# A list scheduler's model of the core: table loads, scan time, exponential pace and latencies changed, and the work ordered anew

## The chip, the cores and the metric

The kernel runs on all eight cores of one Trainium2 chip. Each core computes one of the eight batch elements with the same program; the cores exchange nothing. The metric is the device time of the slowest core, in microseconds (us). Cores 0 to 3 lie on one die and cores 4 to 7 on the other.

For every run there is the span of each core and the mean clock that was granted to its TensorE (1.0 is full speed). In some runs some cores were granted less (0.934 to 0.952 on four in one of the kernel before); the slowest core then tells of the clock.

Engines: PE is TensorE (PEld its weight loads), ACT is ScalarE, DVE is VectorE, POOL is GpSimd, SP issues the DMAs.

## The reference

A hybrid decoder layer, cut to what matters:

```python
D_MODEL = 1024; BATCH = 8; SEQ = 4096
h = rms_norm(x, g_pre); proj = h @ w_in                  # 5648 columns
# mixer A: causal differential attention with ALiBi, 4 heads, two 64-wide maps per head
pd = softmax(s1) - lam * softmax(s2); oa = pd @ v
ya = (rms_norm(oa) * silu(za)) @ w_up_a
# mixer B: gated linear attention (GLA), 4 heads; the decay is the "gate" of this document
glog = log_sigmoid(lr @ w_alpha + b_alpha) / 16
b = cumsum(glog) within a chunk; exp(b), exp(-b) scale q and k
yb = (rms_norm(ob) * silu(zb)) @ w_up_b
y = sigmoid(gate_a) * ya + sigmoid(gate_b) * yb
out = x + rms_norm(y @ w_out, g_post)
```

## The kernel before

The kernel works through eight tiles of 512 tokens. It isn't written as one sequence for each engine. It declares some 15,000 operations, each with a guess of its time (`occ`, how long it holds its engine, and `tail`, how long after that its result is there), and a greedy list scheduler puts them in order, picks an engine where there is a choice, and writes one fixed instruction queue per engine. On the chip each queue ran in that one order, with waits on semaphores: in the trace of the kernel before, the 1169 instructions of ACT, the 2272 of DVE and the 303 of POOL come in the same order on all eight cores. A wrong guess costs nothing by itself; it costs when it puts something in front of a queue that is not ready (3.58 us of PE in the example below).

The core of the scheduler:

```python
SEM_LAT = 0.14
...
        while len(order) < len(ops):
            best = None
            for e in ENGS:
                for o in avail[e]:
                    st = o.ready if o.ready > free[e] else free[e]
                    if len(o.alts) > 1 and any(max(o.ready, free[a]) + o.alts[a][0] < st + o.alts[e][0] for a in o.alts):
                        continue                     # another engine would finish it earlier
                    # ... (cut: buffers) ...
                    key = (st, o.prio, o.idx)        # earliest start first, then priority
                    if best is None or key < best[:3]:
                        best = (st, o.prio, o.idx, o, e)
            # ... (cut) ...
            occ, tail = o.alts[e]
            if e == "pe" and o.mode != pe_mode:
                st += 0.1                            # change of the array's tiling mode
                pe_mode = o.mode
            o.eng, o.start = e, st
            free[e] = st + occ
            o.fin = free[e] + tail                   # (cut: DMAs)
            # ... when the last dependency d of s is placed:
                        if d.eng == "pe" and "pe" in s.alts:
                            t = d.start
                        else:
                            t = d.fin + SEM_LAT
```

The times, and a copy that may go to DVE or to ACT:

```python
def _dve(n, rate=1.0, scalars=0):
    return (0.068 + 0.06 * scalars + n / rate / 960.0, 0.095)
def _act(n, psum=False):
    return ((0.051 if psum else 0.093) + n / 1200.0, 0.115)
...
copy(lambda t=t, s=s: hT[t % 2][:, :, s * 128:(s + 1) * 128], lambda b=b: ptr(b), [b], [f"hT{t % 2}_{s}"], 1024, bf_in=True)   # engs=("dve", "act")
```

The GLA gate, once per tile, is a serial piece (lambdas cut):

```python
P.op({"act": _act(512, True)}, ... func=AF.Exp, scale=-1.0, bias=nbal ...)      # twice
P.op({"act": _act(1024)},      ... func=AF.Ln, bias=1.0 ...)
P.op({"dve": _dve(512)},       ... tensor_tensor_scan ...)                      # twice
P.op({"act": _act(1024)},      ... func=AF.Exp, scale=-1.0 / 16.0 ...)
P.op({"act": _act(1024)},      ... func=AF.Exp, scale=1.0 / 16.0 ...)
```

All the sigmoids and silus are Tanh activations. In the trace below (core 5) Exp follows Tanh 127 times and Ln five times without a table load, but between Tanh and Ln there is always one, of 1283 ns: every tile but the first has a load before its Ln, and every tile has one before the next Tanh. Two PSUM buffers (`pg`) carry all projections, so PE stops when ACT or DVE is late in reading one: on this core it waited 5.1 us in eight waits until DVE had read one into `szB` (L643), and 2.4 us in five until it had at L904.

The softmax here doesn't subtract the row's maximum and nothing guards it: scores larger than these inputs give would overflow.

## Time and profile before

The median of the first three runs is 1463.7 us (1461.4 to 1464.9). The profiled run is fast, with all eight cores between 1448.2 and 1456.4 us at a clock of 0.987 to 0.991.

The first lines of the page (busy time, share of the span, instruction count) of the kernel before, slowest core, core 5:

```profile
span 1456.4 us, 31339 instructions; the slowest of 8 cores (1448.2 to 1456.4 us)
...
PE 1368.1 (94%) x11280; PEld 757.7 (52%) x11280; DVE 771.0 (53%) x2272; ACT 848.8 (58%) x1169; POOL 203.8 (14%) x303
...
PE 85%; DVE 5%; issue 3%; DMA 3%; ACT 3%; POOL 0%; SPq 0%; DVEq 0%; ACTq 0%; POOLq 0%
```

The last line is the chain of waits by engine. PE bounds the kernel, and a busy PE hides stalls inside its busy time (1368 us busy, against 1323 us of pure issue in the table below). So I went through the matmul records one by one: from the start of one to the start of the next, less columns/2.4 GHz + 2.5 ns and 95 ns when the tiling mode changes. The remainder is what I call stall. The three constants are read from this trace: 216 ns for 512 columns and 56 ns for 128, so 2.4 columns a ns and 2.5 ns; and 312 ns in place of 216 (median) after 512 columns when a 64-row matmul comes next, so about 95 ns for the change of mode.

| core 5, before | us |
|---|---|
| pure issue of 11280 matmuls, with 623 mode changes (59 us) | 1323 |
| stall, all | 113 |
| of it in the first 150 us | 34 |
| of it after 1340 us | 18 |
| of it in eight stretches of 14 us, from 3 us before each Ln | 39 |
| of it in single stalls of 1 us or more (28 of them) | 47 |

The groups of instructions of the kernel before, with operation, count, busy time and mean ns of one. They give the table loads, the scan and the exponential:

```profile
L814 ACT ACTIVATE sb_PT<-ps_qk 128x1024 bf16<-128x1024 f32 x480 | 472.0, 1022 | 198.6 <-PE ps_qk L806 194.1 <-PE ps_acc L486 3.5
...
L642 ACT ACT_TABLE_LOAD x8 | 10.3, 1283 | 2.3 <-PE ps_pg L486 2.2
L697 ACT ACT_TABLE_LOAD x7 | 9.0, 1283 | 0.2
...
L700 DVE TENSOR_TENSOR_SCAN sb_cum<-sb_rmask,sb_gl 128x512 f32<-128x512 bf16 x16 | 18.7, 1211 | 10.1 <-ACT sb_gl L697 10.1
```

The sixteenth load is the first instruction of ACT (L623), and the first Ln has none before it. Fifteen loads come from the change between Ln and Tanh: they are gone in e7, where Ln is replaced by Tanh. After each of the 16 loads the next activation starts 11 or 12 ns later, so a load holds ACT for about 1.30 us (387.85 to 389.15 us below). Now the gate of the third tile in order of time (start, length, engine, line, operation; in brackets how long the engine sat idle and what ended it). First ACT, then PE, of the kernel before, core 5:

```profile
387.85 1.28 ACT L697 ACT_TABLE_LOAD   x1
389.15 1.06 ACT L697 ACTIVATE sb_gl<-sb_gl 128x1024 f32<-128x1024 f32 x1
390.22 1.28 ACT L642 ACT_TABLE_LOAD   x1
391.52 0.60 ACT L642 ACTIVATE sb_tmp<-ps_pg 128x512 f32<-128x512 f32 x1
392.01 1.02 ACT L814 ACTIVATE sb_PT<-ps_qk 128x1024 bf16<-128x1024 f32 x1
392.91 1.03 ACT L478 ACTIVATE sb_hT<-ps_pg 128x1024 bf16<-128x1024 bf16 x1
393.82 1.07 ACT L702 ACTIVATE sb_gl<-sb_cum 128x1024 f32<-128x1024 f32 x1
```

```profile
389.56 0.96 PE L486 MATMUL ps_acc<-sb_V,sb_PT 128*128 128x129 bf16 x14
394.09 1.24 PE L486 MATMUL ps_pg<-sb_wbuf,sb_hT 128*128 128x512 bf16 x5 [3.58 <-ACT sb_hT L478]
395.17 3.54 PE L486 MATMUL ps_pg<-sb_hT,sb_wbuf 128*128 128x512 bf16 x8
398.49 0.68 PE L486 MATMUL ps_pg<-sb_wbuf,sb_hT 128*128 128x512 bf16 x2
```

PE waits 3.58 us for a copy into `hT`, which stands in ACT's queue behind Ln, a second table load, a Tanh and an exponential. The model thought that ACT would be free two table loads earlier and gave it the copy. After the wait eight matmuls take 3.54 us, that is 427 ns from one to the next instead of 216: the clock record of this core is 0.5 from 395.2 to 398.7 us.

The same eight stretches, as a table by stretch (busy us and instructions of PE, PEld, DVE, ACT and POOL, then granted clock, share of DMA and GB/s) of the kernel before, four of the eight rows and the sum of all eight:

```profile
386.00:400.00 14.00, 10.43 (x81) 5.44 (x79) 8.54 (x22) 11.20 (x14) 2.16 (x3) 0.88 0.36 128
...
724.00:738.00 14.00, 10.52 (x73) 5.39 (x72) 6.79 (x20) 11.85 (x14) 1.74 (x3) 0.88 0.19 71
910.00:924.00 14.00, 9.94 (x89) 5.50 (x87) 7.08 (x20) 11.75 (x14) 2.20 (x3) 0.89 0.13 53
1110.00:1124.00 14.00, 10.19 (x106) 6.15 (x104) 5.12 (x8) 13.18 (x15) 0.64 (x1) 1.00 0.15 63
...
sum 112.00, PE 86.36 PEld 45.77 DVE 63.99 ACT 87.90 POOL 12.66; mean PE 10.79 PEld 5.72 DVE 8.00 ACT 10.99 POOL 1.58
```

The first number after the length, 14.00, is PE: 10 to 10.5 us of 14 are busy in these four (10.8 in the mean of all eight), in a kernel where PE is busy 94% of the time. A clock of 0.88 means that a quarter of the stretch ran at half (0.5 from 395.2 to 398.7 us in the first row, from 733.2 to 736.6 in the second).

### The profile page before, as it was taken

The page shows a single profiled execution, that of the slowest core. Times are in us where ns is not written, and L with a number is a line of the kernel's source. Part 1 is how long each engine was busy: PE and PEld are TensorE (multiplying, and loading weights), DVE is VectorE, ACT ScalarE, POOL GpSimd, SP SyncE. Part 2 cuts the span into 40 slices and gives each one's busy share as a digit, 9 for nine tenths or more (in the row PEclk, how much of TensorE's full clock was granted, in tenths as well). Part 3 has the DMA queues.
Part 4 walks back from the last instruction along what each step waited for, and adds up shares of the span by engine and source line. Part 5 has one row for each costly group of instructions (what it writes and reads, how often), then busy time and mean ns, then how long its engine had stood idle before and what let it go on. Part 6 is the DMA issues. An engine that isn't in the chain of part 4 may idle for free.

```text
span 1456.4 us, 31339 instructions; the slowest of 8 cores (1448.2 to 1456.4 us)
## 1 busy us (share of the span) xinstructions
PE 1368.1 (94%) x11280; PEld 757.7 (52%) x11280; DVE 771.0 (53%) x2272; ACT 848.8 (58%) x1169; POOL 203.8 (14%) x303
## 2 busy tenths in 40 slices
PE   4997898999899999999999999899998999999896
PEld 2344444545455555555555555466555666655532
DVE  4589567645665465644565435563354543334734
ACT  4356455436644466546765667656677667777511
POOL 1025121101110021101111111010010110101100
PEclk9999999999999999999999999999999999999998
DMA  9999795243523253333512335222243221224133
GB/s 275 291 275 258 228 315 181 80 153 146 174 89 144 88 214 108 114 136 131 198 59 106 113 111 206 76 88 88 88 160 131 88 88 59 88 88 146 59 145 116
DMA packets 54279, 207.54 MB, mean 143 GB/s; under 512 B 6880, under 2 KB 15472, under 8 KB 39152
## 3 DMA queue, kind: packets, MB, share of 16 engines
q1 hardware_dynamic: 54128, 205.54, 41.4%
q8 instruction: 93, 1.52, 0.4%
q14 instruction: 58, 0.48, 0.1%
HBM read 173.01 MB, written 32.51 MB: 141 GB/s over the span
## 4 chain that ended last, share of the span: by engine, by line
PE 85%; DVE 5%; issue 3%; DMA 3%; ACT 3%; POOL 0%; SPq 0%; DVEq 0%; ACTq 0%; POOLq 0%
PE ps_pg L486 57%; PE ps_acc L486 16%; PE ps_qk L806 9%; PE ps_pg L490 2%; DMA sb_KT<-w_out 1%; ACT sb_PT L814 1%; DMA sb_wbuf<-wsc 1%; DVE sb_gatedB L777 1%; ACT L642 1%; DVE sb_cum L700 0%; DMA sb_KT<-w_up_a 0%; DVE sb_junkd L768 0%; DMA sb_xa<-x 0%; DVE sb_szB L643 0%; DVE sb_xr L934 0%
## 5 line engine op out<-in xcount | busy, mean ns | idle before, releaser
L814 ACT ACTIVATE sb_PT<-ps_qk 128x1024 bf16<-128x1024 f32 (+1 forms) x544 | 518.9, 997 | 215.7 <-PE ps_qk L806 209.8
L486 PE MATMUL ps_pg<-sb_hT,sb_wbuf 128*128 128x512 bf16 x1664 | 448.5, 387 | 10.3 <-DVE sb_V L523 1.8
L486 PE MATMUL ps_acc<-sb_V,sb_PT 128*128 128x129 bf16 x4224 | 427.9, 220 | 10.3 <-ACT sb_PT L814 6.8
L486 PEld LDWEIGHTS ps_acc<-sb_V,sb_PT 128*128 128x128 bf16 x4224 | 312.9, 98 | 148.4 <-issue 40.3
L486 PE MATMUL ps_pg<-sb_wbuf,sb_hT 128*128 128x512 bf16 x960 | 247.0, 382 | 13.6 <-ACT sb_hT L478 5.5
L486 PEld LDWEIGHTS ps_pg<-sb_hT,sb_wbuf 128*128 128x128 bf16 x1664 | 155.0, 99 | 161.0 <-issue 45.2
L904 DVE SCALAR_TENSOR_TENSOR sb_tmp<-sb_tmp,ps_pg 128x512 f32<-128x512 f32 x128 | 87.6, 685 | 212.2 <-PE ps_acc L486 138.4
L806 PE MATMUL ps_qk<-sb_QT,sb_KT 64*128 64x256 bf16 (+1 forms) x2176 | 162.6, 268 | 4.9 <-ACT sb_PT L814 4.7
L889 ACT ACTIVATE sb_tmp<-ps_pg 128x512 f32<-128x512 f32 x128 | 76.5, 598 | 108.7 <-PE ps_pg L486 71.9
L486 PEld LDWEIGHTS ps_pg<-sb_wbuf,sb_hT 128*128 128x128 bf16 x960 | 88.0, 98 | 98.8 <-issue 26.3
L486 PE MATMUL ps_pg<-sb_wbuf,sb_yT 128*128 128x512 bf16 x480 | 122.6, 386 | 5.0 <-DMA sb_wbuf<-wsc 3.4
L858 POOL TENSOR_TENSOR sb_statE<-sb_statE,sb_mhalf 128x1 f32<-128x1 f32 x128 | 76.0, 599 | 358.3 <-DVE sb_statE L856 344.9
L806 PEld LDWEIGHTS ps_qk<-sb_QT,sb_KT 64*128 64x128 bf16 x2176 | 83.9, 94 | 73.3 <-issue 55.9
L819 POOL TENSOR_SCALAR_AFFINE_SELECT sb_PT<-sb_PT 128x512 bf16<-128x512 bf16 x64 | 44.8, 700 | 507.4 <-ACT sb_PT L814 507.4
L642 ACT ACTIVATE sb_tmp<-ps_pg 128x512 f32<-128x512 f32 x64 | 38.1, 597 | 67.3 <-PE ps_pg L486 39.6
L486 PEld LDWEIGHTS ps_pg<-sb_wbuf,sb_yT 128*128 128x128 bf16 x480 | 44.3, 99 | 53.8 <-issue 16.0
L486 PE MATMUL ps_pg<-sb_gaT,sb_wbuf 128*128 128x512 bf16 x240 | 71.4, 379 | 0.5 <-DMA sb_wbuf<-wsc 0.5
L486 PE MATMUL ps_pg<-sb_gbT,sb_wbuf 128*128 128x512 bf16 x240 | 69.1, 379 | 0.6 <-DVE sb_tmp L904 0.3
L922 ACT ACTIVATE sb_junk<-ps_pg 128x512 bf16<-128x512 f32 x64 | 38.2, 597 | 48.1 <-PE ps_pg L486 37.6
L925 DVE TENSOR_TENSOR sb_tmp<-ps_pg,sb_gpost 128x512 f32<-128x512 f32 x64 | 44.0, 688 | 34.6 <-ACT sb_junk L922 34.4
L860 DVE SCALAR_TENSOR_TENSOR sb_gatedA<-sb_oaf,sb_statE,sb_szA 128x128 bf16<-128x128 f32 x128 | 45.4, 360 | 22.0 <-POOL sb_statE L858 20.6
L934 DVE SCALAR_TENSOR_TENSOR sb_xr<-sb_tmp,sb_statF,sb_xr 128x512 f32<-128x512 f32 x64 | 45.9, 758 | 20.2 <-DMA sb_xr<-x 13.0
(137 smaller groups left out, 1303.4 us busy)
## 6 DMA issues: line engine op xcount, KB each, us to landing
sb_wbuf<-wsc SPq DMA_DIRECT2D x100, 1024.0 KB, 5.0
sb_KT<-w_in SPq DMA_DIRECT2D x88, 256.0 KB, 9.0
sb_xr<-x SPq DMA_DIRECT2D x36, 512.0 KB, 4.2
out<-sb_xr SPq DMA_DIRECT2D x32, 512.0 KB, 3.1
sb_xa<-x SPq DMA_DIRECT2D x28, 512.0 KB, 5.2
wsc<-sb_wbuf SPq DMA_DIRECT2D x9, 1024.0 KB, 9.1
wsc<-sb_V SPq DMA_DIRECT2D x6, 1024.0 KB, 10.0
sb_KT<-w_out SPq DMA_DIRECT2D x16, 256.0 KB, 8.3
```

The costliest lines, as they stand in the source:

```text
L486: return P.op(_pe(n), lambda e: e.matmul(out=out_f(), lhsT=lf(), rhs=rf(), start=start, stop=stop, **kw), reads=reads, writes=writes, mode ...
L642: P.op({"act": _act(512, True)}, lambda e: e.activation(out=tmp[z.i][:], in_=pg[b.i][:], func=AF.Tanh, scale=0.5), reads=[b], writes=[z])
L806: lambda e, kb=kb, m=m, kbi=kbi, ca=ca, n=n: e.matmul(out=qk[:, 2 * half + m, kbi * 256:kbi * 256 + n], lhsT=KT[64 * m:64 * m + 64, h, kb ...
L814: P.op({"act": _act(2 * width, True)}, lambda e: e.activation(out=PT[pt.i][:, :, 0:width], in_=qk[:, 2 * half:2 * half + 2, 0:width], func ...
L819: return e.affine_select(out=v, in_=v, pattern=[[0, 2], [0, 2], [1, 128]], compare_op=ALU.is_ge, fill=0.0, base=0, channel_multiplier=-1)
L858: P.op({"pool": (0.45, 0.1)}, lambda e: e.tensor_tensor(out=statE[st.i][:, 4:5], in0=statE[st.i][:, 3:4], in1=mhalf[:, 0:1], op=ALU.pow), ...
L860: P.op({"dve": _dve(128, 1.0, 1)}, lambda e: e.scalar_tensor_tensor(out=gatedA[:, blk, h * 128:(h + 1) * 128], in0=oaf[o2.i][:], scalar=st ...
L889: P.op({"act": _act(512, True)}, lambda e, b=b, z=z: e.activation(out=tmp[z.i][:], in_=pg[b.i][:], func=AF.Tanh, scale=0.5), reads=[b], wr ...
L904: P.op({"dve": _dve(512)}, lambda e, b=b, z=tg[ab]: e.scalar_tensor_tensor(out=tmp[z.i][:], in0=tmp[z.i][:], scalar=1.0, in1=pg[b.i][:], o ...
L922: P.op({"act": (0.571, 0.02)}, lambda e, b=b, st=st, hh=hh: e.activation(out=junk[:, hh, :], in_=pg[b.i][:], func=AF.Square, accum_out=sta ...
L925: P.op({"dve": _dve(512)}, lambda e, b=b, z=z, hh=hh: e.tensor_tensor(out=tmp[z.i][:], in0=pg[b.i][:], in1=gpost[:, hh * 512:(hh + 1) * 51 ...
L934: P.op({"dve": _dve(512, 1.0, 1)}, lambda e, hh=hh, xb=xb, st=st, z=zs[hh]: e.scalar_tensor_tensor(out=xr[xb.i][:, hh * 512:(hh + 1) * 512 ...
```

## The change

The intent: let the scheduler's model know what the trace shows, so that the order it writes fits the machine. No instruction is added or taken away; only the order and the choice between engines change. The diff, cut to its core:

```diff
-SEM_LAT = 0.14
+SEM_LAT = 0.15
...
+            if e == "act" and o.table is not None and o.table != table:
+                st += 1.29
+                table = o.table
             o.eng, o.start = e, st
...
                         if d.eng == "pe" and "pe" in s.alts:
                             t = d.start
+                        elif "pe" in s.alts:
+                            t = d.fin + 0.11
                         else:
                             t = d.fin + SEM_LAT
...                                    (in the normalisation)
-                P.op({"dve": _dve(1024, 2.0)}, ...
+                P.op({"dve": _dve(1024, 2.0, 1)}, ...
...                                    (twice, at both kinds of Tanh; Ln gets table="ln")
-  func=AF.Tanh, scale=0.5), reads=[b], writes=[z])
+  func=AF.Tanh, scale=0.5), table="tanh", reads=[b], writes=[z])
...                                    (the gate's first Exp, and its scan)
-                P.op({"act": _act(512, True)}, ...
+                P.op({"act": (0.57, 0.115)}, ...
-                P.op({"dve": _dve(512)}, lambda e, c=c: e.tensor_tensor_scan(...
+                P.op({"dve": (1.12, 0.095)}, lambda e, c=c: e.tensor_tensor_scan(...
...                                    (the attention's exponential and its mask)
-                P.op({"act": _act(2 * width, True)}, ...
+                P.op({"act": (0.075 + width / 600.0, 0.1)}, ...
-                    P.op({"pool": (0.594, 0.05)}, tri, reads=[pt], writes=[pt])
+                    P.op({"pool": (0.7, 0.05)}, tri, reads=[pt], writes=[pt])
```

The load's 1.29 us is added after the operation has been chosen. The scheduler doesn't avoid a load; everything that it places later sees ACT busy for longer.

More of the change, by code (lines that the diff above doesn't have):

```diff
@@ L48 @@
 class _Op:
-    __slots__ = ("eng", "alts", "fn", "deps", "bufs", "is_dma", "sem", "val", "needs_inc", "prio", "idx", "mode", "atom",
+    __slots__ = ("eng", "alts", "fn", "deps", "bufs", "is_dma", "sem", "val", "needs_inc", "prio", "idx", "mode", "atom", "table",
                  "stream", "pre", "nleft", "succ", "start", "fin", "ready", "nbytes")
@@ L82, in buf, with op @@
         return _Buf(pool, self.made[pool] - 1)
-    def op(self, alts, fn, reads=(), writes=(), dma=None, nbytes=0, mode=None, atom=None, claim=(), after=()):
+    def op(self, alts, fn, reads=(), writes=(), dma=None, nbytes=0, mode=None, atom=None, claim=(), after=(), table=None):
         o = _Op()
@@ L90, in op @@
         o.sem, o.val, o.needs_inc = dma, 0, o.is_dma
-        o.idx, o.mode, o.atom = len(self.ops), mode, atom
+        o.idx, o.mode, o.atom, o.table = len(self.ops), mode, atom, table
         o.stream = self.stream
@@ L146, in schedule @@
         lock_left = 0
-        pe_mode = None
+        pe_mode = table = None
         atoms = {}
@@ L629, in stage_a @@
                      reads=[(st, 1), "mhalf"], writes=[(st, 2)])
-                P.op({"dve": _dve(1024, 2.0)}, lambda e, xb=xb, h=h, st=st: e.tensor_scalar(out=hb[h.i][:, :], in0=xa[xb.i][:], scalar1=statA[st.i][:, 2:3],
+                P.op({"dve": _dve(1024, 2.0, 1)}, lambda e, xb=xb, h=h, st=st: e.tensor_scalar(out=hb[h.i][:, :], in0=xa[xb.i][:], scalar1=statA[st.i][:, 2:3],
                                                                                        scalar2=None, op0=ALU.mult),
@@ L641, in silu @@
             tm(w, t, s, b, claim=[z], after=[f"{key}{s}"])
-            P.op({"act": _act(512, True)}, lambda e: e.activation(out=tmp[z.i][:], in_=pg[b.i][:], func=AF.Tanh, scale=0.5), reads=[b], writes=[z])
+            P.op({"act": _act(512, True)}, lambda e: e.activation(out=tmp[z.i][:], in_=pg[b.i][:], func=AF.Tanh, scale=0.5), table="tanh", reads=[b], writes=[z])
             P.op({"dve": _dve(512)}, lambda e: e.scalar_tensor_tensor(out=dst[:, s, :], in0=tmp[z.i][:], scalar=1.0, in1=pg[b.i][:], op0=ALU.add,
@@ L694, in stage_glaproj @@
                 mm(lambda b=b: pg[b.i][:], walpha[:, c * 128:(c + 1) * 128], lrT[:, :], True, True, 512, ["walpha", "lrT"], [b], mode="row32", after=[f"gl{c}"])
-                P.op({"act": _act(512, True)}, lambda e, c=c, b=b: e.activation(out=gl[:, c, :], in_=pg[b.i][:], func=AF.Exp, scale=-1.0,
+                P.op({"act": (0.57, 0.115)}, lambda e, c=c, b=b: e.activation(out=gl[:, c, :], in_=pg[b.i][:], func=AF.Exp, scale=-1.0,
                                                                               bias=nbal[:, c:c + 1]), reads=[b, "nbal"], writes=[f"gl{c}"])
-            P.op({"act": _act(1024)}, lambda e: e.activation(out=gl[:, :, :], in_=gl[:, :, :], func=AF.Ln, bias=1.0, scale=1.0),
+            P.op({"act": _act(1024)}, lambda e: e.activation(out=gl[:, :, :], in_=gl[:, :, :], func=AF.Ln, bias=1.0, scale=1.0), table="ln",
                  reads=["gl0", "gl1"], writes=["gl0", "gl1"])
             for c in range(2):
-                P.op({"dve": _dve(512)}, lambda e, c=c: e.tensor_tensor_scan(out=cum[:, c, :], data0=rmask[:, :], data1=gl[:, c, :], initial=0.0,
+                P.op({"dve": (1.12, 0.095)}, lambda e, c=c: e.tensor_tensor_scan(out=cum[:, c, :], data0=rmask[:, :], data1=gl[:, c, :], initial=0.0,
                                                                            op0=ALU.mult, op1=ALU.add), reads=[f"gl{c}", "rmask"], writes=[f"cum{c}"])
@@ L813, in qk_pair @@
                 c = SLOPES[h] * 256.0 * (i - U) + EXP_SHIFT
-                P.op({"act": _act(2 * width, True)}, lambda e: e.activation(out=PT[pt.i][:, :, 0:width], in_=qk[:, 2 * half:2 * half + 2, 0:width],
+                P.op({"act": (0.075 + width / 600.0, 0.1)}, lambda e: e.activation(out=PT[pt.i][:, :, 0:width], in_=qk[:, 2 * half:2 * half + 2, 0:width],
                                                                            func=AF.Exp, bias=c, scale=1.0), reads=[f"qk{half}"], writes=[pt])
@@ L888, in stage_e @@
                     fm(wg, t, col, b, claim=[z], last=[f"gates{t}"] if j == 7 and ab == 1 else [])
-                    P.op({"act": _act(512, True)}, lambda e, b=b, z=z: e.activation(out=tmp[z.i][:], in_=pg[b.i][:], func=AF.Tanh, scale=0.5),
+                    P.op({"act": _act(512, True)}, lambda e, b=b, z=z: e.activation(out=tmp[z.i][:], in_=pg[b.i][:], func=AF.Tanh, scale=0.5), table="tanh",
                          reads=[b], writes=[z])
```

## The prediction

> **What bounds the kernel now.** The page gives PE 94% busy (1368 of 1456 us), ACT 58%, DVE 53%, POOL 14%; the chain of waits is 85% PE. From the matmul records (start to next start, less columns/2.4 GHz + 2.5 ns and 95 ns per change of tiling mode), I count some 1323 us of pure issue, 59 us of it 623 mode changes, and 113 us in which PE did not issue at pace. Only the 113 us can be won by a new order: 34 us in the first 150 us (DMA 91 to 95% busy), 18 us after 1340 us (tail), and 39 us in eight stretches of 14 us, from 3 us before each tile's GLA gate Ln.
>
> **What happens there.** The timeline at 387 to 399 us: a table load of 1.28 us, the Ln 1.06, two scans of 1.21 each on DVE, a second load before the next tanh. The fixed order comes from a model with free loads and a scan of 0.70 us, so ACT and DVE run late. PE waits 3.6 us at 394 us for an ACT copy; then matmuls go at 427 ns instead of 216 ns for 3.5 us, 1.5 us lost. Four of seven later tiles show it. [...]
>
> **What the change does.** No instruction is added or removed. The 16 table loads (20.5 us of ACT) stay. [...] The added terms fit the trace: load 1.29, scan 1.12+0.095 against 1.21, exponential 0.928 start to start against 0.920 (0.904 before), affine select 0.70 against 0.70. The latency edits don't: ACT or DVE to PE measures 0.145 us (old 0.14, new 0.11), PE to ACT 0.10 (0.14, now 0.15). The load's penalty is added after an operation is chosen, so loads aren't avoided, only allowed for: copies can go to DVE, and PE gets other work.
>
> **On the critical path.** All of the 39 us is PE stall, but two PSUM buffers for projections and the serial gate (load, Ln, scans, two exps, about 7 us) keep some. I expect half to go, about 18 us with half of the slow-clock stretches (3 us) in it, 2 us elsewhere, and 2 us lost to random reordering (mode changes may move 3 us either way).
>
> Estimate: 1463.7 - 18 - 2 + 2 = 1446 us; range 1433 to 1459. Chances: faster by over 2% 0.10, within 2% 0.88, slower by over 2% 0.02.
>
> **What would show it.** Right: 16 table loads; busy sums of ACT, DVE, POOL within 1%; PE idle time from 88 us to about 70; long PE waits on ACT and DVE next to the Ln mostly gone, fewer 427 ns matmuls; the stretches around the Ln at 20 us stall; first 150 us and tail within 4 us of before. Wrong in the reason: same stalls at the Ln, but fewer mode changes or a shorter start or tail.
>
> **What would make it wrong.** List order is chaotic: a tie broken otherwise can give back 10 us anywhere. The optimistic 0.11 us could put PE before unready work hundreds of times, 30 to 40 ns each. If the gate's chain can't be hidden, nothing is gained.

They held no term of the sum, which stays as it was: 1463.7 - 18 - 2 + 2 = 1446 us. That half of the half-clock stretches would go with the waits, some 3 us within the 18, was my estimate, from the four such stretches between 200 and 1340 us in the trace of core 5.

## The result, and the profile after

| | before | after, first runs | after, repeated (e5 below) |
|---|---|---|---|
| runs (all), median us | 1463.35 (4) | 1451.5 (4) | 1437.1 (5) |
| ratio of the fast runs, 95% interval | | 0.9917 (0.9897 to 0.9936) | 0.9834 (0.9819 to 0.9849) |
| undisturbed cores, us | 1452.7 (one run); 1454.8 in the later rounds | 1432.8 | 1429.5 |

The first result was 0.8% faster, and the repeat 1.7%. The difference is in the cores. This is the list of the cores of the first profiled run of the kernel after (span and granted clock):

```profile
core 0: 1423.1 us, clock 0.993
core 1: 1431.8 us, clock 0.993
core 2: 1450.2 us, clock 0.976
core 3: 1445.4 us, clock 0.973
core 4: 1427.7 us, clock 0.993
core 5: 1435.1 us, clock 0.989
...
```

Cores 2 and 3 have a lower clock: the clock record of core 2 is 0.812 from 47 to 209 us, but for 3.4 us, and 1.0 from there almost to the end. Every fast one of these first runs had such a pair, and the slowest core is one of the pair. In the repeat no core was below 0.990 in any of the five runs. So the profile after is read on core 5, which was not slowed and has all 11280 matmul records, as core 5 of before had. Its sums, from the table by stretch over the whole span (PE, PEld, DVE, ACT, POOL, clock):

```profile
0.00:1436.00 1436.00, 1362.34 (x11280) 758.71 (x11280) 773.88 (x2273) 849.22 (x1168) 198.90 (x303) 0.99 0.43 145
```

The work is the same. The gate of the third tile after, first ACT, then PE, then one line of DVE:

```profile
388.39 1.28 ACT L702 ACT_TABLE_LOAD   x1
389.69 1.06 ACT L702 ACTIVATE sb_gl<-sb_gl 128x1024 f32<-128x1024 f32 x1
390.76 1.28 ACT L647 ACT_TABLE_LOAD   x1
392.06 0.60 ACT L647 ACTIVATE sb_tmp<-ps_pg 128x512 f32<-128x512 f32 x1
392.55 1.94 ACT L819 ACTIVATE sb_PT<-ps_qk 128x1024 bf16<-128x1024 f32 x2
```

```profile
390.10 0.96 PE L491 MATMUL ps_acc<-sb_V,sb_PT 128*128 128x129 bf16 x14
391.20 1.89 PE L491 MATMUL ps_pg<-sb_wbuf,sb_hT 128*128 128x512 bf16 x8
394.03 1.89 PE L491 MATMUL ps_pg<-sb_wbuf,sb_hT 128*128 128x512 bf16 x8 [0.94 <-DVE sb_statE L850]
395.85 0.61 PE L811 MATMUL ps_qk<-sb_QT,sb_KT 64*128 64x256 bf16 x8
```

```profile
390.37 0.69 DVE L484 COPY sb_hT<-ps_pg 128x1024 bf16<-128x1024 bf16 x1 [0.36 <-PE ps_acc L491]
```

The table loads are all still there, of the same length and in the same place. But the copy into `hT` is now on DVE, at 390.37 us and ahead of the scans, as it should be when the model knows that ACT is taken. PE gets this operand 3 us earlier and no longer waits for it. The longest wait left here is 0.94 us, for another operand (`statE` from DVE), in place of 3.58, and no slow stretch follows (eight matmuls in 1.89 us). The counterparts of the four stretches shown of before, and the sum of all eight:

```profile
387.00:401.00 14.00, 12.79 (x105) 6.94 (x103) 11.13 (x26) 12.12 (x15) 2.17 (x3) 1.00 0.30 113
...
717.00:731.00 14.00, 12.06 (x105) 6.68 (x106) 7.91 (x22) 13.26 (x16) 1.74 (x3) 1.00 0.16 64
900.00:914.00 14.00, 11.97 (x103) 6.55 (x101) 9.03 (x23) 12.95 (x15) 2.20 (x3) 1.00 0.06 23
1096.00:1110.00 14.00, 12.82 (x109) 7.12 (x109) 7.65 (x14) 13.13 (x15) 0.64 (x1) 1.00 0.10 42
...
sum 112.00, PE 95.83 PEld 51.79 DVE 71.21 ACT 93.33 POOL 12.08; mean PE 11.98 PEld 6.47 DVE 8.90 ACT 11.67 POOL 1.51
```

PE is busy 12 to 12.8 us of 14 in place of about 10.3, and the clock is 1.00 in all four. These four gained most. Of the other four, the last gained too (11.73 to 13.44 us), the first and the fourth stayed (10.37 to 10.35 and 11.45 to 11.55), and the second got worse (11.75 to 10.85); the mean of all eight rises from 10.79 to 11.98 us. Counted over core 5: single stalls of 1 us or more fall from 28 (47.3 us) to 19 (29.4 us), while stalls of 15 to 100 ns stay (about 100 of them, some 5 us, in both). Stall in the Ln stretches falls from a median of 38.6 us (six cores of before with full records) to 22.2 us (five undisturbed cores of after) and 20.1 us (repeat). It also shows in earlier starts: on core 5 the third Ln comes at the same time as before, the fourth 5 us sooner, the fifth 7, the sixth 11, the seventh 15, the eighth 17.

### The profile page after: what moved, and what is told of

Its sections match the earlier page's. It is cut to its first block, busy times and chain, and to the rows that moved or that the text cites. A ratio compares the mean times of both kernels' runs of the same rounds, so it can differ in the third digit from the quotient of the medians.

```text
span 1450.2 us, 31152 instructions; the slowest of 8 cores (1423.1 to 1450.2 us)
## 1 busy us (share of the span) xinstructions
PE 1361.1 (94%) x11086; PEld 764.5 (53%) x11280; DVE 772.7 (53%) x2273; ACT 848.3 (58%) x1168; POOL 198.7 (14%) x303
## 4 chain that ended last, share of the span: by engine, by line
PE 84%; DMA 4%; DVE 4%; issue 4%; ACT 3%; SPq 1%; POOL 0%; DVEq 0%; ACTq 0%; POOLq 0%
PE ps_pg L491 57%; PE ps_acc L491 16%; PE ps_qk L811 9%; DMA sb_wbuf<-wsc 2%; PE ps_pg L495 2%; ACT sb_PT L819 1%; DMA sb_KT<-w_in 1%; DMA sb_KT<-w_up_a 1%; ACT sb_tmp L647 0%; DVE sb_xr L939 0%; DVE sb_cum L705 0%; SPq L561 0%; DVE sb_szB L648 0%; DMA sb_xr<-x 0%; DVE sb_gatedB L782 0%
## 5 line engine op out<-in xcount | busy, mean ns | idle before, releaser
L491 PE MATMUL ps_pg<-sb_hT,sb_wbuf 128*128 128x512 bf16 x1583 | 429.8, 388 | 11.1 <-DVE sb_wbuf L568 2.9
L491 PE MATMUL ps_pg<-sb_wbuf,sb_hT 128*128 128x512 bf16 x906 | 239.6, 388 | 11.2 <-DVE sb_statE L861 1.8
L491 PE MATMUL ps_pg<-sb_wbuf,sb_yT 128*128 128x512 bf16 x456 | 114.2, 379 | 7.1 <-DMA sb_wbuf<-wsc 4.3
L491 PE MATMUL ps_pg<-sb_gbT,sb_wbuf 128*128 128x512 bf16 x221 | 64.5, 382 | 1.8 <-issue 0.7
L930 DVE TENSOR_TENSOR sb_tmp<-ps_pg,sb_gpost 128x512 f32<-128x512 f32 x64 | 44.1, 689 | 36.1 <-ACT sb_junk L927 35.9
L939 DVE SCALAR_TENSOR_TENSOR sb_xr<-sb_tmp,sb_statF,sb_xr 128x512 f32<-128x512 f32 x64 | 45.6, 753 | 25.3 <-DMA sb_xr<-x 17.8
```

The lines of the kernel that those rows point to most:

```text
L491: return P.op(_pe(n), lambda e: e.matmul(out=out_f(), lhsT=lf(), rhs=rf(), start=start, stop=stop, **kw), reads=reads, writes=writes, mode ...
L930: P.op({"dve": _dve(512)}, lambda e, b=b, z=z, hh=hh: e.tensor_tensor(out=tmp[z.i][:], in0=pg[b.i][:], in1=gpost[:, hh * 512:(hh + 1) * 51 ...
L939: P.op({"dve": _dve(512, 1.0, 1)}, lambda e, hh=hh, xb=xb, st=st, z=zs[hh]: e.scalar_tensor_tensor(out=xr[xb.i][:, hh * 512:(hh + 1) * 512 ...
```

## The experiments

e1 to e4, e5 to e8 and e9 to e12 were three jobs, each on a chip of its own and with its own runs of the kernel before. The edits of the change are independent of each other, so they can be put in apart; e1 and e2 together make up the whole change. "Undisturbed" is the median of cores at a clock of 0.985 or more, and the number after it the difference to the same measure of the kernel before on the same chip (1456.3 us in the first job, 1454.8 in the second, 1455.8 in the third). "Ln stall" is the stall in the eight stretches, median of the cores that were undisturbed and had full records.

| run | what it is | ratio of fast runs (95%) | undisturbed us | Ln stall us |
|---|---|---|---|---|
| before | | 1 | | 38.6 |
| e1 | loads + scan only | 0.9887 (0.9862 to 0.9912) | 1438.8, -17.5 | 23 |
| e2 | the other edits only | 0.9962 (0.9941 to 0.9982) | 1449.9, -6.4 | 35 |
| e3 | all but the latencies | 0.9881 (0.9861 to 0.9901) | 1437.6, -18.7 | 23 |
| e4 | all, load 1.33 for 1.29 | 0.9852 (0.983 to 0.9874) | 1432.8, -23.5 | 22 |
| e5 | the change again | 0.9834 (0.9819 to 0.9849) | 1429.5, -25.3 | 20 |
| e6 | loads only | 0.9903 (0.9887 to 0.9918) | 1439.6, -15.2 | 26 |
| e7 | before, no Ln | 0.9864 (0.9849 to 0.9879) | 1433.4, -21.4 | 22 |
| e8 | after, no Ln | 0.9786 (0.9773 to 0.9799) | 1422.7, -32.1 | 15 |
| e9 | all, but 0.15 to PE | 0.9897 (0.986 to 0.9935) | 1439.4, -16.4 | 25 |
| e10 | all, measured latencies | 0.9933 (0.9895 to 0.9971) | 1442.5, -13.3 | 24 |
| e11 | all, plus tail load | 0.9839 (0.979 to 0.9889) | 1427.5, -28.3 | 21 |
| e12 | e11 with 0.08 to PE | 0.9892 (0.9854 to 0.9931) | 1434.2, -21.6 | 22 |

All results were correct, except e7 and e8. Their outputs are wrong, which doesn't matter for the times. My theory, G: the gain is the gate. The queues of ACT and DVE no longer meet two table loads (1.28 us each) and a slow scan (1.21 us, 0.60 in the model) that the order had not allowed for. The rivals: P, the exponential's pace or the latencies did it; C, a greedy order is chaotic, and any new one differs by chance.

### e1 to e4: which edits, and how much is chance

e1, the kernel before with these two edits:

```diff
+            if e == "act" and o.table is not None and o.table != table:
+                st += 1.29
+                table = o.table
-                P.op({"dve": _dve(512)}, lambda e, c=c: e.tensor_tensor_scan(...
+                P.op({"dve": (1.12, 0.095)}, lambda e, c=c: e.tensor_tensor_scan(...
```

> The model of the kernel before plus only two of the edits: table loads of 1.29 us and the scan's 1.12 us. Theory G (the gain is the gate: ACT and DVE queues no longer surprised at the Ln): spans of cores at a granted clock of 0.985 or more near 1432 us (before 1452, after 1429), stall in the eight 14 us stretches around the Ln about 22 us (before 39, after 22). Theory P (the exponential's pace, the latencies or the affine select made the gain): spans 1445 to 1452, Ln stretches still 35 or more. Theory C (any new list order differs by chance): anything from 1425 to 1460, with no relation to the Ln stretches.

e2, the whole change without those two:

```diff
 (e2 = after, with)
-            if e == "act" and o.table is not None and o.table != table: ...
-                P.op({"dve": (1.12, 0.095)}, lambda e, c=c: e.tensor_tensor_scan(...
+                P.op({"dve": _dve(512)}, lambda e, c=c: e.tensor_tensor_scan(...
```

> The complement: exponential pace, latencies, affine select and the scalar term of the normalisation, but loads free and the scan at 0.60 us as before. Theory G: undisturbed cores at 1447 to 1454 us, Ln stretches 35 to 42 us. Theory P: undisturbed cores near 1432, Ln stretches near 22 us. Theory C: no relation.

e1 gives 17.5 us on undisturbed cores and brings the Ln stall from 38.6 to 23 us; e2 gives 6.4 us and leaves it at 35. The spans of e1 came out some 7 us above what I had written for theory G, those of e2 within it. The two add up: 17.5 + 6.4 = 23.9, against 25.3 for the whole (e5) and 23.5 for the whole with a nudge (e4). So the gate is some 70% of the gain, and there is a second part that theory G hadn't foreseen.

e3, the whole change without the latency edits:

```diff
 (e3 = after, with)
-SEM_LAT = 0.15
+SEM_LAT = 0.14
-                        elif "pe" in s.alts:
-                            t = d.fin + 0.11
```

> The whole change but for the latency edits (0.14 kept, no 0.11 for TensorE's consumers), which fit the trace worse than the old value. Theory G: undisturbed cores at 1424 to 1432 us (after 1429), Ln stretches 18 to 24 us; the latencies do nothing. Theory P with the latencies as its cause: 1445 to 1452.

e3 is at 1437.6, 1.2 us from e1. So the other edits (the pace of both exponentials, the affine select and the normalisation) together bring about 1 us, which is less than the nudge of e4 will move, and the rest of the second part, 5 to 7 us, is the latencies. That lies between what the two theories said; "the latencies do nothing" is wrong.

e4, a nudge of the changed kernel:

```diff
-                st += 1.29
+                st += 1.33
```

> The changed kernel with the load at 1.33 us in place of 1.29: a nudge without meaning, to measure how far chance moves the order. Theory G: undisturbed cores within 4 us of 1429, Ln stretches 19 to 25 us. Theory C: 1429 plus or minus 10 or more. On the clock: if the reordered kernel itself draws two or four cores to a granted clock near 0.81 between 47 and 209 us, this one shows it in most of its runs and the kernel before, on the same chip, in few; if it is the chip's own state, both show it alike.

e4 has 1432.8 us undisturbed, -23.5 against its own before; the unaltered change has -25.3 on its chip. The nudge did change the order: in the profiles of the two, only 440 of ACT's 1152 instructions and 10682 of PE's 11280 have the same names and shape at the same place. Yet it moved the time by 2 us at most, across two chips. So theory C in its strong form is unlikely, though one nudge is a small sample. Of the clock: none of the three fast runs here had the lowered pair (one run that counts as slow had it, at 0.967).

### e5 to e8: the change again, the loads alone, and the loads taken away

e5 is the changed kernel, unaltered.

> The changed kernel unaltered, once more. In its first rounds all three fast runs had two cores at a granted clock of 0.974 to 0.976. Theory S (the clock is the chip's state, not the order's doing): most fast runs here have all eight cores at 0.985 or more, and the ratio of the fast runs is 0.983 to 0.987 in place of 0.9917. Theory O (the new order draws the lower clock): two cores near 0.975 in most fast runs again, ratio near 0.992. Undisturbed cores near 1433 us in both.

e5 answers as theory S said: ratio 0.9834, all cores at 0.990 or more in all five runs. The change's own effect is 1.7% and the first 0.8% was pressed down by the two slowed cores.

e6, the kernel before with the table loads in the model alone (the first three lines of the diff of e1).

> The kernel before plus the table loads alone in the model; scan still 0.60 us. With loads and scan together the undisturbed cores went from 1456.3 to 1438.8. Theory T (the loads are most of it, 2 x 1.29 us against 2 x 0.52 us of scan per tile): undisturbed cores at 1440 to 1446. Rival (the scan is most of it[...]): 1450 to 1455.

e6 takes 15.2 us, a little beyond its range (1439.6, expected 1440 to 1446). The loads are most of the gate's part. The scan's 2 us (17.5 in e1 against 15.2 here, on two chips) is no more than the nudge of e4 moved, so its part isn't shown.

e7 and e8 turn the question round. They leave each order alone and take the loads away on the machine:

```diff
-  func=AF.Ln, bias=1.0, scale=1.0), ...
+  func=AF.Tanh, bias=1.0, scale=1.0), ...
```

> The kernel before in its own order, with Tanh in place of Ln: wrong results on purpose, same durations, and 14 or 15 of the 16 table loads gone. It makes the machine agree with the old model in this one point. Theory G: undisturbed cores fall from 1456 to 1437 to 1444 us, most of what the reordering for the loads won. Rival (the order gained by chance): falls only by what ACT is saved off the chain, 1450 to 1455.

> The same edit in the changed order, which already allows for the loads. Theory G: it gains little, 3 to 9 us from 1433, so undisturbed cores at 1424 to 1430, less than half of what the same edit gives in the old order. Rival (the order has nothing to do with the loads): it gains as much as in the old order.

The groups of ACT show a single load in both. This is that line of e7, core 0:

```profile
L623 ACT ACT_TABLE_LOAD x1 | 1.3, 1283 | 7.6 <-DMA sb_xa<-x 7.6
```

In the old order this gains 21.4 us, more than I had written (12 to 19). In the new order it gains 1429.5 - 1422.7 = 6.8 us, within the 3 to 9 that I had written. The same fifteen loads, 15 x 1.283 = 19.2 us of ACT, cost 21.4 us where the order doesn't know of them and 6.8 us where it does. The difference, 14.6 us, is what e6 gained by telling the model (15.2 us). This is the strongest support of theory G for the loads, by a way that needs no new order: knowing hides about two thirds of their cost, and the remaining third is there as before. One reserve: the order of e8 differs from that of e7 by all the edits and not by the loads alone.

### e9 to e12: the latencies, and a tail

Measured from the trace, the time from the end of an ACT instruction to the start of a PE instruction that waited for it is 0.144 us (median), from DVE to PE 0.147, from PE to ACT 0.096, from ACT to DVE 0.10. The old model's 0.14 was right for PE; the change makes PE's 0.11 (too early) and the others' 0.15 (too late).

e9:

```diff
-                            t = d.fin + 0.11
+                            t = d.fin + 0.15
```

> The changed kernel, but what TensorE reads is ready 0.15 us after its producer's end, as for all other engines, in place of 0.11 (measured 0.144). Without both latency edits the ratio was 0.9881, with both 0.9834. Theory W (the optimistic 0.11 is what gains: the greedy choice then waits some 30 ns for the more urgent matmul rather than starting another): ratio 0.987 to 0.990. Rival V (the general 0.15, which makes the other engines' work look later, gains): ratio 0.982 to 0.985. Theory C (chance of the list order): anything, and the next run tells.

e10:

```diff
-SEM_LAT = 0.15
+SEM_LAT = 0.10
-                            t = d.fin + 0.11
+                            t = d.fin + 0.145
```

> The changed kernel with the latencies that the trace shows: 0.145 us from ACT or DVE to TensorE, 0.10 to the others. If a truer model always gives a better order: ratio below 0.9834. Theory W (TensorE's consumers gain by optimism): 0.986 to 0.990. Theory V: 0.986 to 0.990 too, so this run and the one before tell V from W together.

e11, against a wait that both profiles show near the end. PE of the changed kernel, core 5:

```profile
1404.74 0.81 PE L491 MATMUL ps_pg<-sb_gbT,sb_wbuf 128*128 128x512 bf16 x3
1408.77 17.44 PE L491 MATMUL ps_pg<-sb_wbuf,sb_yT 128*128 128x512 bf16 x64 [3.22 <-DMA sb_wbuf<-wsc]
```

```diff
-            wo = [acquire(W_O), acquire(W_O + 1)]
+            wo = [acquire(W_O)]
+            if t < ntiles - 1:
+                wo.append(acquire(W_O + 1))
+            else:                                # KT[:, 0, :] holds head 0's keys, no longer read
+                wk_ = _Fixed()                   # stands for a buffer at KT[:, 0, :]
+                P.op({"sp": (0.38, 0.0)}, lambda e: e.dma_start(out=KT[:, 0, :], in_=wsc[W_O + 1]), ...
+                wo.append(wk_)
```

> The changed kernel, with the last output weight chunk of the last tile loaded into the key buffer of head 0, which is free by then, in place of a weight buffer that comes free late. In both profiles TensorE waits 3.4 to 3.7 us for that load at about 20 us before its end and then runs some 3 us at half pace. Expected: that wait gone, undisturbed cores 3 to 6 us faster than the changed kernel, ratio 0.979 to 0.982. Rival: the tail is held by the serial chain of normalisation and stores, and nothing is gained.

e12 is e11 with 0.08 in place of 0.11.

> The kernel of the run before with 0.08 us in place of 0.11 for TensorE's consumers. Theory W if more optimism helps further: another 1 to 4 us, ratio 0.977 to 0.981. If 0.11 was past the useful point or chance: the same or up to 5 us slower than the run before.

e9 loses 9 us against the change and so speaks for theory W (the 0.11, not the 0.15, gains). Its ratio of 0.9897 is in W's range, but with the help of two of its six runs, which had a lowered clock; the other four give 0.9866, just below that range and above V's. Its Ln stall is 25 us against 20. But e12 speaks against W: 0.08 costs 6.7 us against e11 of the same job, where more optimism should have gained and the rival allowed up to 5. And e10, the latencies as measured, is the slowest of all variants that know the loads (1442.5 us). Its ratio, 0.9933, is beyond what any theory said; two of its five fast runs had a lowered clock. So over five settings the undisturbed time moves by 12 us without a rule that I could find: 0.14/0.14, 0.15/0.15, 0.15/0.11, 0.10/0.145, and 0.15/0.08 (the last with the tail load of e11). That 0.11 is the best of the five is shown; why is not. It may be a tuned point of a choppy landscape. A nudge of the load's time moved it by only 2 us, so not every small edit scatters like this. It stays open.

e11 does what it should at the place. PE of e11, core 1:

```profile
1408.38 1.02 PE L495 MATMUL ps_pg<-sb_gbT,sb_wbuf 128*128 128x512 bf16 x4
1411.35 1.02 PE L495 MATMUL ps_pg<-sb_wbuf,sb_yT 128*128 128x512 bf16 x4 [1.95 <-DVE sb_yT L915]
1412.21 1.03 PE L495 MATMUL ps_pg<-sb_KT,sb_yT 128*128 128x512 bf16 x4
```

The wait is 1.95 us, now for DVE, and groups of four matmuls take their 1.02 us with no half-clock stretch. Undisturbed cores are 3 us faster than those of the change (28.3 against 25.3), at the lower edge of what was expected and across two chips. By the chip's time it isn't shown: its ratio is 0.9839 with a wide interval, because three of its five fast runs had two or more cores at 0.974 to 0.977. Its two runs without such cores took 1432.9 and 1433.7 us; the five of e5 took 1435.5 to 1440.1. I would keep it, with that reserve.

### The clock: what stays open

On the third chip the lowered clock (0.970 to 0.979 on a pair of cores or more) came in none of the nine fast runs of the kernel before, and in 11 of the 22 runs of e9 to e12 that were not deeply slow. On the chips of the first two jobs it came in none of the fast runs of any kernel, but in all three fast ones of the very first runs of the kernel after. The old kernel isn't free of it: one slow run in the first job (1480.3 us) had a pair at 0.962 and 0.968. The profiles of e5, e6 and e8 hold it for some 5 us only, at 0.812 on all four cores of one die about 50 us in (in e6 again at 169 us on two of them); the kept profiles of before, e2 and e7, whose orders don't know the loads, have none, but nor have those of e1, e3, e4, e9 and e12. So on some chips the reordered kernels may draw it more often than the old one. In the profile of after it lies in the first 210 us, which hold only the first tile's gate. How many cores it takes in differs: in that profile two cores of die 0 had a mean clock of 0.993 beside the 0.976 and 0.973 of the pair, while in one slow run of e10 all four cores of a die had 0.817 to 0.820. In 42 of the 69 runs of after and e1 to e12 no core was below 0.985. No experiment told the reason.

## Why the prediction was right or wrong

The time lay in the range (1433 to 1459) in the first runs and in the repeat. The estimate, 1446, was too high for the undisturbed change by some 9 us and too low for the first runs by 5.5. That the first number came so near owes something to chance: a gain larger than foreseen and a slowed pair of cores partly cancelled.

- "Only the 113 us can be won by a new order": right. Pure issue is the same within about 1 us (some 1323 us on both cores 5), with 630 mode changes against 623. The gain is in long stalls, 47 to 29 us.
- "39 us in eight stretches ... I expect half to go": right. It is 22 us in the first profile and 20 in the repeat. "Long PE waits next to the Ln mostly gone" holds from the third tile on: stalls of 1 us or more in the stretches of core 5 fall there from 10 to 3, but in the first two tiles they go from 4 to 5.
- "PE idle time from 88 us to about 70": right on comparable cores, 66 to 73 us in the first profile; the slowed core can't be compared.
- "copies can go to DVE, and PE gets other work": right; the `hT` copy at 390 us shows the first half.
- "16 table loads", "first 150 us and tail within 4 us": right. On core 5 the first 150 us have 35.9 us of stall against 34.2, the tail 14.8 against 18.2. "busy sums of ACT, DVE, POOL within 1%": right for ACT and DVE; POOL's fell by 2.4% (203.8 to 198.9 on core 5; 203.1 to 204.3 over the eight cores before, 198.7 to 200.3 after).
- "fewer 427 ns matmuls": right. Between 200 and 1340 us core 5 has 28 of them (512 columns, 415 to 440 ns) before and 2 after. The clock record of core 5 has four half-clock stretches there before, and none after; over all eight cores it is 3 to 6 before and 0 to 2 after.
- The term that was mis-sized is the remainder, "2 us elsewhere, and 2 us lost to random reordering". It held the latency edits, which I counted as nothing because they fit the trace worse. They brought 5 to 7 us, for a reason that stays open. With them the sum is 17.5 for the gate, about 1 for exponential, select and normalisation and some 6 for the latencies, 25 us in place of 18.
- "The optimistic 0.11 us could put PE before unready work hundreds of times": this did not happen. Stalls of 15 to 100 ns are as many as before (about 100).
- The other thing I hadn't counted is the clock. The metric is the slowest core, and the first runs gave it to a slowed pair. The first runs lost about half of the gain in this way (ratio 0.9917 against 0.9834).

Of the half clock, the trace shows this. On core 5 of before, the one PE wait of over 3 us near a gate (3.58 us) was followed by a stretch at half clock (395.2 to 398.7 us), but so was one of 2.40 us (559.1 to 562.5 us), and so were two of 1.50 and 1.88 us close together (733.2 to 736.6 us). One of 1.97 us on core 5 of after, at 551 us, was not. What sets the half clock off is not shown.

## What to carry to other kernels

When a static order is made by a model, look for the events that the model has at zero, such as a table load (1283 ns here) or an instruction form that takes twice as long (the scan here, 1.21 us against 0.60 in the model), and look at PE's longest waits beside them; telling the model of them hid two thirds of their cost here without touching an instruction. Check each correction on its own, because a more exact latency may make a greedy order worse (e10: 1442.5 us undisturbed, against 1429.5 of the change), and meaningless nudges tell how much chance there is. And where the metric is the slowest of eight cores, read the clock of each core before believing a difference of one per cent.
